# Two more products by seven from chunk 2 on, a new order, and a one-column clear on GpSimd behind each accumulating DMA

## The chip, the cores and the metric

The kernel runs on one core of a Trainium2 chip. The metric is the device time of one execution in microseconds (us); a median of several executions stands for a kernel. The engines of the core are called as in the profile: PE (TensorE, matmuls; PEld is its weight load), DVE (VectorE), ACT (ScalarE), POOL (GpSimd) and SP (SyncE, which issues most DMAs). SBUF is the on-chip memory, PSUM the memory, in banks, into which PE writes its sums.

## The reference

One layer of a gated short-convolution mixer between two RMS norms, in float32. x is 1024 x 1024, `w_in` 1024 x 8192, `w_out` 2048 x 1024.

```python
def short_conv_mixer(u, w_in, conv_w, w_out):
    z, bg, cg, v = jnp.split(u @ w_in.astype(u.dtype), 4, axis=-1)
    y = bg * causal_dwconv(cg * v, conv_w) * jax.nn.silu(z)
    return y @ w_out.astype(u.dtype)

# DEPTH = 1, one short-convolution layer
u = rms_norm(x, pre_norm)
h = x + rms_norm(short_conv_mixer(u, w_in, conv_w, w_out), post_norm)
```

The convolution is causal over the positions, three taps wide, each of the 2048 channels for itself. The other mixer of the file isn't used at this depth.

## The kernel before

**Products by seven.** Both large matrix products are computed as 2 x 2 blocks with seven block products in place of eight (Strassen's scheme in Winograd's form), named a, b, c, e, d, f, g. For `u @ w_in` the work goes by pairs p and chunks c: chunk c has the pairs 2c and 2c+1, sixteen chunks in all. Each float32 operand is split into a high part (rounded to the type fp32r) and a low part (the rest), and each block product is three matmuls: low by high, high by low, high by high. A plain product (`product`) is 12 matmuls of 512 columns. Its weights are tiles named by the letter: `wdh` and `wdl` are the high and the low part for product d, `wch` and `wcl` for c, and so on; the u side lies in tiles such as `u_d`.

**Seven again.** Products b, f and g can be taken by the same scheme once more, over the two pairs of a chunk together: two plain products (24 matmuls of 512 columns) become seven small ones, a' to g', of 6 matmuls of 256 columns (`deep_product`, 42 matmuls). `by_seven(z, c)` says whether product z of chunk c goes so: b from chunk `DEEP` on, f from `DEEP_F`, g from `DEEP_G`, each up to the last chunks. Before, these are 2, 3 and 4. The results go to PSUM tiles such as `px2b`, `pv2f`, `px2g`, which DVE adds to the sums `sna`, `snc`, `sne` in SBUF.

What the small products need: once for the whole kernel the u side, that is, for each of b, f and g eight subtractions on POOL (`deep_subs`, in tiles `deepb`, `deepf`, `deepg`) and the splits of four operands c', e', d', g' (`deep_split`, into tiles such as `ubch_deep`, `ubcl_deep`); for each chunk four sums of 128 x 256 on the weight side (`deep_sums`, tiles `dsb`, `dsf`, `dsg`) and their splits (`deep_prep`, tiles `dwb1h`, `dwb1l` and so on). The table `UNDER` says at which product of which pair the setups of the u side are recorded.

**Splits by bank.** A split takes ACT for the high part and DVE for the low part. Many go by way of one PSUM bank, `beside`, which all of them use in turn: ACT copies the source to the high part and into the bank, and DVE subtracts the high part from the bank. `split_w` takes this way for the weights of a, d and g in chunks whose f goes by seven; `deep_split` in the setups takes it always.

**Transfers.** For the second large product, sums of `w_out`'s blocks are formed in DRAM (`t_d`): SP copies blocks, and sixteen DMAs with an addition (accumulating DMAs), issued by POOL's queue, add others to them. `sums_plan(p0)` lays them out over the pairs from p0 - 1 on, one accumulating DMA for each pair. `TODO` says with which pairs the `tb` tiles are fetched.

**What sets the order.** From `plan.record()` on nothing is issued at once; each operation is recorded by the class `Plan`, with its tiles and an estimated duration. At the end `flush` gives each a due time (`deadlines`), shifts the due times of some by a table (`PLAN["boost"]`, operation number to microseconds), and lays out the instructions of each engine in the order that this gives (`arrange`; `take` moves some POOL operations to DVE). The order of PE is the recorded one. `emit` then issues them by way of `call`, and so every recorded instruction has the line of `call` in the profile (L288).

Of the kernel before, what the change touches and what calls it, by code (L numbers as in the profile page):

```python
# [19 lines left out]
DEEP = 2  # L20
DEEP_F = 3
DEEP_G = 4
# [619 lines left out]
def kernel(  # L642
# [17 lines left out]
    P = 128  # L660
# [1441 lines left out]
```

## Time and profile before

| | us |
|---|---|
| median of 3 executions | 776.41 (775.64 to 776.58) |
| profiled execution, its own time | 776.59 |
| its span in the profile | 774.8 |
| PE busy | 763.8 (99%) |
| DVE busy | 669.9 (86%) |
| ACT busy | 451.2 (58%) |
| POOL busy | 442.6 (57%) |
| start of chunk 2 (product c of pair 4) | 100.01 |
| start of the output product | 618.90 |

A row of a timeline gives the start and the length of an instruction in us, its engine, line and operation, output<-inputs by the program's names without buffer numbers, and in brackets how long the engine was idle before it and what ended that. "PE px L288 <- DVE wdl L288" in the view of waits reads: PE, about to write `px`, waited for DVE's write of `wdl`; then us in total, how many times, the longest. A row of the view of windows gives for a stretch from:to its length and, for each engine, the busy time and the number of instructions.

### The profile page before, as it was taken

The numbers are of one execution on the slowest core, as the hardware profiler recorded it, in microseconds if no ns is written. First come the engines' busy times: TensorE is split into PE (matmuls) and PEld (weight loads), VectorE is DVE, ScalarE is ACT, GpSimd is POOL, SyncE is SP. The second block draws the span as 40 slices with busy tenths as digits, with TensorE's granted clock in tenths as the row PEclk, the third lists the DMA queues.
The fourth block names the chain that finished last, engine by engine and source line by source line (L and its number), as shares of the span: only waits on it lengthen the run. The fifth ranks groups of instructions, "written<-read, shape, count | busy, mean of one in ns | idle before, by whom it ended". The sixth has DMA issues, their size and how long they took to land.

```text
span 774.8 us, 12631 instructions
## 1 busy us (share of the span) xinstructions
PE 763.8 (99%) x4266; PEld 668.0 (86%) x4266; DVE 669.9 (86%) x1009; ACT 451.2 (58%) x861; POOL 442.6 (57%) x397
## 2 busy tenths in 40 slices
PE   8999999999999999999999999999999999999996
PEld 7888888888988898988888888888888889889885
DVE  6899878786989898999899989797899899977993
ACT  7774456675755565756565656556553656564831
POOL 2518994558695859777788687565637100600321
PEclk9999999999999999999999999999999999999999
DMA  9222432354747575556667673724254998666842
GB/s 315 67 55 55 122 111 80 121 161 146 177 136 171 170 161 146 165 143 191 197 177 212 176 203 94 185 81 140 84 163 131 359 388 278 202 224 212 266 142 108
DMA packets 117136, 130.09 MB, mean 168 GB/s; under 512 B 7320, under 2 KB 74704, under 8 KB 116944
## 3 DMA queue, kind: packets, MB, share of 16 engines
q1 hardware_dynamic: 112560, 120.77, 48.4%
q0 software_dynamic: 4352, 8.39, 7.3%
q8 instruction: 33, 0.54, 0.3%
q14 instruction: 31, 0.25, 0.1%
q10 hardware_dynamic: 160, 0.14, 0.0%
HBM read 101.74 MB, written 44.30 MB: 188 GB/s over the span
## 4 chain that ended last, share of the span: by engine, by line
PE 97%; DVE 1%; issue 1%; DMA 1%; ACT 0%; POOL 0%; DVEq 0%; POOLq 0%; ACTq 0%
PE px L288 40%; PE pv L288 15%; PE po_x L288 11%; PE px2b L288 5%; PE px2f L288 3%; PE po_v L288 3%; PE pp L288 3%; PE px2g L288 3%; PE pv2b L288 2%; PE pv2f L288 2%; PE pf_x L288 1%; PE pb_x L288 1%; PE py2b L288 1%; PE py L288 1%; PE pv2g L288 1%
## 5 line engine op out<-in xcount | busy, mean ns | idle before, releaser
L288 PE MATMUL px<-u_d,wdh 128*128 128x512 f32 x248 | 76.7, 390 | 0.0
L288 PE MATMUL px<-u_a,wah 128*128 128x512 f32 x248 | 76.7, 390 | 0.0
L288 PE MATMUL pv<-u_e,weh 128*128 128x512 f32 x248 | 76.6, 390 | 0.0
L288 PE MATMUL px<-u_c,wch 128*128 128x512 f32 x248 | 76.6, 390 | 0.0
L288 ACT COPY beside<-raw 128x512 f32<-128x512 f32 x64 | 37.9, 592 | 37.5 <-DVE wal L288 13.3
L288 PEld LDWEIGHTS px<-u_d,wdh 128*128 128x128 f32 x248 | 46.6, 188 | 9.1
L288 PEld LDWEIGHTS px<-u_c,wch 128*128 128x128 f32 x248 | 46.7, 188 | 9.1
L288 PEld LDWEIGHTS pv<-u_e,weh 128*128 128x128 f32 x248 | 46.6, 188 | 9.0
L288 PEld LDWEIGHTS px<-u_a,wah 128*128 128x128 f32 x248 | 46.7, 188 | 8.9
L288 ACT COPY sna<-px 128x512 f32<-128x512 f32 x30 | 17.6, 586 | 60.4 <-PE px L288 55.6
L288 DVE SCALAR_TENSOR_TENSOR cv<-gpad,cw,cv 128x1024 f32<-128x1024 f32 x32 | 49.4, 1544 | 2.5 <-ACT cv L288 2.3
L288 PE MATMUL px<-u_d,wdl 128*128 128x512 f32 x124 | 48.8, 393 | 0.7 <-DVE wdl L288 0.7
L288 PE MATMUL px<-u_a,wal 128*128 128x512 f32 x124 | 48.6, 392 | 0.0
L288 PE MATMUL px<-u_c,wcl 128*128 128x512 f32 x124 | 48.5, 391 | 0.0
L288 PE MATMUL pv<-u_e,wel 128*128 128x512 f32 x124 | 48.5, 391 | 0.0
L288 POOL TENSOR_TENSOR sf<-raw,sc 128x512 f32<-128x512 f32 x27 | 41.2, 1524 | 10.8 <-issue 5.5
L288 POOL TENSOR_TENSOR raw<-raw,raw 128x512 f32<-128x512 f32 x31 | 45.2, 1459 | 3.5 <-DVE se L288 2.9
L288 POOL TENSOR_TENSOR sc<-se,raw 128x512 f32<-128x512 f32 x24 | 37.3, 1555 | 15.2 <-PE px L288 4.9
L288 POOL TENSOR_TENSOR se<-raw,raw 128x512 f32<-128x512 f32 x22 | 31.1, 1414 | 23.6 <-DVE sna L288 4.7
L288 POOL TENSOR_TENSOR rs_post<-ve_post,minus_half 128x1 f32<-128x1 f32 x7 | 4.9, 704 | 64.5 <-DVE ve_post L288 64.5
L288 ACT COPY snc<-px 128x512 f32<-128x512 f32 x31 | 18.0, 580 | 26.5 <-PE px L288 26.5
L288 POOL TENSOR_TENSOR sne<-snc,sne 128x512 f32<-128x512 f32 x10 | 13.5, 1346 | 33.7 <-ACT snc L288 31.9
(491 smaller groups left out, 2618.2 us busy)
## 6 DMA issues: line engine op xcount, KB each, us to landing
raw<-in_sc_w_in SPq DMA_DIRECT2D x128, 256.0 KB, 3.8
y_d<-cv SPq DMA_DIRECT2D x16, 512.0 KB, 2.7
s_d<-s SPq DMA_DIRECT2D x32, 256.0 KB, 3.2
t_d<-in_sc_w_out POOLq DMA_DIRECT2D x16, 512.0 KB, 7.9
t_d<-in_sc_w_out SPq DMA_DIRECT2D x16, 256.0 KB, 5.2
tb<-in_sc_w_out SPq DMA_DIRECT2D x16, 256.0 KB, 4.0
t_d<-t_d SPq DMA_DIRECT2D x16, 256.0 KB, 4.7
s<-y_d SPq DMA_DIRECT2D x16, 256.0 KB, 3.1
```

Source lines behind the costliest of these rows:

```text
L288: getattr(engine, name)(*(self.plain(a) for a in args), **{k: self.plain(a) for k, a in kw.items()})
```

## The change

`DEEP_F` and `DEEP_G` go from 3 and 4 to 2: product f of chunk 2 and product g of chunks 2 and 3 are taken by seven too. The setups for f and g move with them, so that all twelve operands of the u side are recorded with the products of chunk 2 (`UNDER`, pairs 4 and 5). `sums_plan(10)` becomes `sums_plan(4)`: the copies and the accumulating DMAs for `t_d` begin with pair 3, and before with pair 9. The `tb` fetches start with pair 7 in place of 9. `emit` issues a clear of a 128 x 1 tile on GpSimd behind each DMA of its queue; the planner doesn't know of it. The table of due times is another one. In all there are 54 more matmuls, 22 more rows on DVE's list, 19 more on ACT's, 26 more on POOL's (16 of them clears) and 4 fewer on SP's.

```diff
 DEEP = 2
-DEEP_F = 3
-DEEP_G = 4
+DEEP_F = 2
+DEEP_G = 2
...
     "boost": {
-        0: 3.28, 1: -1.55, 2: -5.74, 3: -3.49, 4: 0.9, 5: -13.11, 6: -1.63, 7: -10.08, 20: 23.61, 21: 13.96,
...
+        0: 0.65, 1: 1.53, 2: -1.38, 5: 25.25, 6: 0.34, 20: 1.61, 22: 15.9, 25: 0.33, 58: 2.17, 59: 3.37,
...
             self.call(op.name[0], op.engine, op.name[1], op.args, op.kw)
+            if op.engine == "gpsimd" and op.name[1] == "dma_start":
+                self.call(op.name[0], "gpsimd", "memset", (self.mark, 0.0), {})
...
-    sums_plan(2 * DEEP_F + 4)
+    sums_plan(4)
...
         ("e", 2 * DEEP - 1): lambda: deep_subs("b", [0]),
         ("f", 2 * DEEP - 1): lambda: deep_subs("b", [1]),
-        ("d", 2 * DEEP): lambda: (deep_split("b", "c'", True), deep_split("b", "e'", True)),
-        ("f", 2 * DEEP): lambda: deep_subs("f", [0, 1]),
-        ("g", 2 * DEEP): lambda: deep_split("b", "d'", True),
-        ("e", 2 * DEEP + 1): lambda: deep_split("b", "g'", True),
-        ("d", 2 * DEEP_F): lambda: deep_split("f", "c'", True),
-        ("a", 2 * DEEP_F + 1): lambda: deep_split("f", "e'", True),
-        ("g", 2 * DEEP_F): lambda: deep_split("f", "d'", True),
-        ("c", 2 * DEEP_F + 1): lambda: deep_split("f", "g'", True),
-        ("e", 2 * DEEP_G - 2): load_ug,
-        ("e", 2 * DEEP_G - 1): lambda: deep_subs("g", [0]),
-        ("a", 2 * DEEP_G): lambda: deep_subs("g", [1]),
-        ("a", 2 * DEEP_G + 1): lambda: deep_split("g", "c'", True),
-        ("c", 2 * DEEP_G + 1): lambda: deep_split("g", "e'", True),
-        ("e", 2 * DEEP_G + 1): lambda: deep_split("g", "g'", True),
-        ("d", 2 * DEEP_G + 1): lambda: deep_split("g", "d'", True),
+        ("c", 2 * DEEP): lambda: (deep_split("b", "c'", True), deep_split("b", "e'", True)),
+        ("e", 2 * DEEP): lambda: (deep_split("b", "d'", True), deep_subs("f", [0, 1])),
+        ("d", 2 * DEEP): load_ug,
+        ("a", 2 * DEEP + 1): lambda: [deep_split("f", i, True) for i in ("c'", "e'", "d'")],
+        ("c", 2 * DEEP + 1): lambda: (deep_split("b", "g'", True), deep_split("f", "g'", True)),
+        ("e", 2 * DEEP + 1): lambda: deep_subs("g", [0, 1]),
+        ("d", 2 * DEEP + 1): lambda: [deep_split("g", i, True) for i in ("c'", "e'", "g'", "d'")],
     }
...
+    plan.mark = small.tile([P, 1], F32, tag="mark", name="mark", bufs=1)
     plan.record()
```

How the new order differs is shown at two places. The first is DVE in chunk 2 around the low part of product d's weights for the chunk's second pair, pair 5 (`wdl`; the numbers behind the names tell the buffers apart). Before:

```order
L288 TENSOR_TENSOR wel_1162<-se_1062,weh_1113 128x512
L288 TENSOR_TENSOR dwb2l_1191<-dsb_2_1126,dwb2h_1151 128x512
L288 TENSOR_TENSOR sna_987<-px2b_1064,sna_987 128x256
L288 TENSOR_TENSOR sna_1173<-pv2b_1177,sna_1173 128x256
L288 TENSOR_TENSOR wdl_1203<-raw_10_974,wdh_1134 128x512
L288 TENSOR_TENSOR wfl_1207<-sf_1145,wfh_1186 128x512
```

In the same place after the change, with f and g by seven:

```order
L258 TENSOR_TENSOR dwf_2_1286<-sf_1134,dwf_2_1286 128x256
L258 TENSOR_TENSOR ubgl_deep<-beside,ubgh_deep 128x512
L258 TENSOR_TENSOR dsg_2_1317<-raw_11_987 128x256
L258 TENSOR_TENSOR dwg0l_1323<-raw_11_852,dwg0h_1311 128x512
L258 TENSOR_TENSOR ufgl_deep<-beside,ufgh_deep 128x512
L258 TENSOR_TENSOR sna_1018<-pv2b_1205,sna_1018 128x256
L258 TENSOR_TENSOR snc_1055<-pv2f_1271,snc_1055 128x256
L258 TENSOR_TENSOR sna_1200<-px2b_1086,sna_1200 128x256
L258 TENSOR_TENSOR wdl_1359<-beside,wdh_1259 128x512
L258 TENSOR_TENSOR dwg1l_1362<-dsg_2_1317,dwg1h_1356 128x512
```

Now two setup splits by the bank (`ubgl_deep`, `ufgl_deep`), a sum and a split for g, and three reads of small products' results stand directly ahead of `wdl`, which itself comes by the bank and no longer from `raw`. In the later chunks of before, where all three products go by seven, `wdl` stands ahead of those reads; this is chunk 5:

```order
L288 TENSOR_TENSOR dwf_5_2494<-sf_2330,dwf_5_2494 128x256
L288 TENSOR_TENSOR dwg0l_2506<-raw_11_1989,dwg0h_2474 128x512
L288 TENSOR_TENSOR wdl_2514<-beside,wdh_2416 128x512
L288 TENSOR_TENSOR sna_2215<-pv2b_2406,sna_2215 128x256
L288 TENSOR_TENSOR sna_2398<-px2b_2309,sna_2398 128x256
L288 TENSOR_TENSOR snc_2291<-pv2f_2464,snc_2291 128x256
```

Against these rows the three reads and `wdl` of the new chunk 2 stand the other way round. The second place is POOL's list around an accumulating DMA, among the sums of g's weight side (`dsg`). Before, in chunk 5:

```order
L288 TENSOR_TENSOR dsg_5_2486<-raw_11_2185 128x256
L288 DMA t_d<-in_sc_w_out 128x2x512
L288 TENSOR_TENSOR dsg_5_2486<-dsg_5_2486,raw_11_1989 128x256
L288 TENSOR_TENSOR dsg_5_2525<-raw_11_1989,raw_11_2185 128x256
L288 TENSOR_TENSOR dsg_5_2525<-raw_11_1989,dsg_5_2486 128x256
L288 TENSOR_TENSOR se_2547<-raw_10_2422,raw_11_2456 128x512
```

After the change, in chunk 4, where such a DMA stands among the same sums:

```order
L258 TENSOR_TENSOR dsg_4_2210<-raw_11_1896 128x256
L258 DMA t_d<-in_sc_w_out 128x2x512
L258 MEMSET mark 128x1
L258 TENSOR_TENSOR dsg_4_2210<-dsg_4_2210,raw_11_1744 128x256
L258 TENSOR_TENSOR dsg_4_2245<-raw_11_1744,raw_11_1896 128x256
L258 TENSOR_TENSOR dsg_4_2245<-raw_11_1744,dsg_4_2210 128x256
```

The clear stands between the DMA and the operation that stood directly behind it before.

140 rows, old and new, of the table PLAN are left out of this document.

## Prediction

> **What bounds the kernel now.** I read the page's busy times first, then the chain of waits, then the waits of PE (TensorE), then the chunks one by one.
>
> ```profile
> PE 763.8 (99%) x4266; PEld 668.0 (86%) x4266; DVE 669.9 (86%) x1009; ACT 451.2 (58%) x861; POOL 442.6 (57%) x397
> PE 97%; DVE 1%; issue 1%; DMA 1%; ACT 0%; POOL 0%; DVEq 0%; POOLq 0%; ACTq 0%
> PE pv2f L288 <- DVE dwf2l L288: 0.9, 1, 0.9
> PE px L288 <- DVE wdl L288: 0.7, 1, 0.7
> ```
>
> PE works 763.8 of 774.8 us and is 97% of the chain that ended last. The last two rows are all that PE waited between 80 and 620 us, in the whole middle of the kernel: once for `dwf2l`, once for `wdl`, both from DVE. So the time falls by the matmuls taken away and by those two waits, and it rises by each place where DVE, at 86%, comes too late for PE.
>
> The next view gives one row per chunk, from its first product c to the next chunk's: from:to and length, then busy time (instructions) of PE, weight load, DVE, ACT, POOL, then granted clock, DMA share and GB/s. The rows are chunks 2 to 6, and chunk 8.
>
> ```profile
> 100.01:137.74 37.73, 37.73 (x187) 32.02 (x186) 28.40 (x42) 23.27 (x49) 26.62 (x22) 1.00 0.25 79
> 137.74:175.07 37.33, 37.33 (x206) 32.50 (x204) 28.62 (x47) 25.69 (x53) 20.12 (x20) 1.00 0.48 149
> 175.07:210.53 35.46, 35.46 (x211) 31.57 (x210) 29.33 (x46) 22.90 (x51) 26.87 (x26) 1.00 0.57 151
> 210.53:249.58 39.05, 37.41 (x224) 33.08 (x223) 35.60 (x50) 21.53 (x43) 29.05 (x27) 1.00 0.58 167
> 249.58:286.50 36.92, 36.92 (x224) 32.99 (x223) 33.15 (x50) 21.26 (x41) 27.67 (x26) 1.00 0.63 162
> 323.40:360.30 36.90, 36.90 (x224) 32.96 (x223) 34.64 (x52) 22.53 (x43) 25.82 (x27) 1.00 0.56 159
> ```
>
> Each product taken by seven shortens a chunk (37.73 with b, 37.33 with b and f, 36.90 with all three; chunk 4 is short because the g of its last pair ends in chunk 5). Only chunk 5 loses: 39.05 against 36.92. DVE can be busy 34.64 of 36.90 us, 94%, and PE still loses nothing.
>
> **The change part by part.** *Matmuls.* Product f of chunk 2 and g of chunks 2 and 3 go by seven: three more. The chain's pieces price them:
>
> ```profile
> 107.04 2.75 PE px L288 x12
> 109.79 2.72 PE pv L288 x12
> 105.61 0.71 PE px2b L288 x6
> 640.66 2.87 PE pb_x L288 x24
> ```
>
> A plain product of 12 matmuls of 512 columns is 2.72 to 2.75 us; a small one, 6 of 256 columns, 0.71, and 24 matmuls of that size take 2.87, 120 ns each, 0.72 for 6. Two plain products (5.47, a 2.75 and a 2.72) become seven small ones (7 x 0.72 = 5.04): 0.40 to 0.43 each time. From the chunks it is the same: chunks 2 to 5 without chunk 5's loss are 37.73 + 37.33 + 35.46 + 36.92 = 147.44, and the new pattern is 35.46 + 3 x 36.90 = 146.16. That is **-1.28 us**, all on PE's path, with 54 more matmuls (4320). The Trainium skill (TensorE: Matmul & The Clock Gate, Back-to-back issue gap) gives N/2.4 + 2.5 ns for a matmul at full clock, by which 24 of 512 columns against 42 of 256 would save 0.59 us each time, 1.8 in all, and the sum below would be 0.5 lower. The trace's 120 ns against 109 for the small ones decides for 1.28.
>
> *Chunk 5's loss.* Here are DVE, then POOL (GpSimd), then PE in that stretch; the columns are start, length, engine, work.
>
> ```profile
> 231.99 3.25 DVE L288 TENSOR_TENSOR dwb<-raw,dwb 128x256 fp32r<-128x256 f32 x1
> 235.16 0.68 DVE L288 TENSOR_TENSOR dwf2l<-beside,dwf2h 128x512 fp32r<-128x512 f32 x1
> 235.76 0.89 DVE L288 TENSOR_TENSOR dwf<-sf,dwf 128x256 fp32r<-128x256 f32 x1
> 236.57 1.77 DVE L288 TENSOR_TENSOR dwg0l<-raw,dwg0h 128x512 fp32r<-128x512 f32 x1
> 238.27 0.68 DVE L288 TENSOR_TENSOR wdl<-beside,wdh 128x512 fp32r<-128x512 f32 x1
> ...
> 230.41 1.15 POOL L288 DMA_DIRECT2D t_d<-in_sc_w_out  x1
> 231.16 1.17 POOL L288 TENSOR_TENSOR dsg<-dsg,raw 128x256 f32<-128x256 f32 x1
> 231.87 1.15 POOL L288 TENSOR_TENSOR dsg<-raw,raw 128x256 f32<-128x256 f32 x1
> 232.57 1.14 POOL L288 TENSOR_TENSOR dsg<-raw,dsg 128x256 f32<-128x256 f32 x1
> ...
> 235.89 0.39 PE L288 MATMUL pv2f<-u_f,dwf2l 128*128 128x256 f32 x1 [0.90 <-DVE dwf2l L288]
> 239.00 0.50 PE L288 MATMUL px<-u_d,wdl 128*128 128x512 f32 x1 [0.74 <-DVE wdl L288]
> ```
>
> `dwb`, a subtraction of two SBUF tiles, takes 3.25 us, through three POOL operations on end, all begun without a gap behind an accumulating DMA that POOL issues. What follows on DVE is late: `dwf2l` ends at 235.84 and `wdl` at 238.95, and PE starts 0.05 us after each. The 0.90 and 0.74 and 0.49 of slowed matmuls make 2.13 (39.05 - 36.92). The same subtraction took 0.41 in the next chunk, where another operation was caught behind the next such DMA:
>
> ```profile
> 269.82 1.16 POOL L288 DMA_DIRECT2D t_d<-in_sc_w_out  x1
> ...
> 271.96 2.01 DVE L288 TENSOR_TENSOR dsg<-raw,raw 128x256 f32<-128x256 f32 x1
> 273.89 0.41 DVE L288 TENSOR_TENSOR dwb<-raw,dwb 128x256 fp32r<-128x256 f32 x1
> ...
> 342.77 1.82 DVE L288 TENSOR_TENSOR dwb<-raw,dwb 128x256 fp32r<-128x256 f32 x1
> ```
>
> The last row is the third such case, two chunks on; behind the other thirteen of these DMAs I find none as long.
>
> After the change a clear of one column stands between the DMA and the POOL operation behind it. It reads no tile, and I take it that DVE gets its turn there; and the order around every such DMA is new besides. So **-2.13**, with ends 0 (the hold stays and again meets a thin place) and -2.13. The Trainium skill (SBUF — State Buffer, Who interferes with whom) says that a DVE instruction with two SBUF inputs contends with a GpSimd instruction that reads SBUF, and not with one that only writes; that agrees with `dwb` here, but a lock for one instruction would hold it for 1.17, not 3.25.
>
> *The clears themselves.* The nearest row is a clear of the same size in the head:
>
> ```profile
> 0.74 0.10 POOL L288 MEMSET eps_t<- 128x1 f32 x1 [0.29 <-POOLq L2088]
> 95.43 1.12 DVE L288 TENSOR_TENSOR wcl<-sc,wch 128x512 fp32r<-128x512 f32 x1 [1.84 <-ACT wch L288]
> 100.01 0.39 PE L288 MATMUL px<-u_c,wcl 128*128 128x512 f32 x1
> ```
>
> Sixteen of 0.10 us are 1.6 us of POOL, which is idle 43% of the span: 0. If a clear waited for the DMA's issue (1.15 us) POOL would lose 18 us, still under its 332 idle us. The accumulating DMAs and SP's copies ahead of them come three chunks earlier, the fetches for `tb` one: DMA engines are 0.25 busy in chunk 2 and 0.63 in chunk 6 without a wait of PE, so 0 too; on POOL's queue each puts 0.7 us (230.41 to 231.16) ahead of `dsg` and `se`, which POOL has spare time for (26.62 of 37.73 busy in chunk 2).
>
> *The crowded chunk 2.* All twelve setups of the small products' u sides, before spread over chunks 2, 3 and 4, now lie in chunk 2. In the new order three DVE reads of product b's and f's results stand ahead of `wdl` of the chunk's second pair. The last of them reads what the small product d' of b leaves; that product is over at 24.22 us from the chunk's start by PE's own pace, and product d, which needs `wdl`, is due at 24.94. Reads start 0.19 us behind the end of the product, as here:
>
> ```profile
> 230.85 0.42 DVE L288 TENSOR_TENSOR snc<-px2f,snc 128x256 f32<-128x256 f32 x1 [1.80 <-PE px2f L288]
> ```
>
> That product's successor began at 230.66. Then 0.34 for the read, 0.68 for `wdl`, 0.05 to PE: 24.22 + 1.26 = 25.48, a wait of 0.54 that no speed elsewhere removes. Above it counts DVE's work. The groups of DVE between 100 and 500 us, with mean ns, price its rows:
>
> ```profile
> L288 DVE SCALAR_TENSOR_TENSOR cv<-gpad,cw,cv 128x1024 f32<-128x1024 f32 x20 | 30.6, 1532 | 0.8 <-ACT cv L288 0.6
> L288 DVE TENSOR_TENSOR wel<-se,weh 128x512 fp32r<-128x512 f32 x21 | 19.9, 948 | 0.3 <-POOL dsb L288 0.3
> L288 DVE TENSOR_TENSOR dwb<-raw,dwb 128x256 fp32r<-128x256 f32 x11 | 9.1, 824 | 0.3 <-ACT dwb L288 0.3
> L288 DVE TENSOR_TENSOR sna<-px2b,sna 128x256 f32<-128x256 f32 x43 | 17.8, 414 | 6.0 <-PE px2b L288 6.0
> ```
>
> From the chunk's start to that `wdl` stand 45 DVE rows: 19 of 512 columns that read PSUM (0.68, as `wdl` above) and 10 of 256 (0.41), 8 and 7 that read SBUF alone (0.95 and 0.8), one convolution tap (1.53): 12.9 + 4.1 + 7.6 + 5.6 + 1.5 = 31.75 in all; less 0.08 of overlap each, 28.15. DVE has 24.94 plus its lead, 3.46 us (`wcl` ends at 96.55, PE takes it at 100.01): 28.4. At the 94% that chunk 8 showed, 28.15 becomes 29.95, a wait of 1.5; at 85%, 33.1, one of 4.7. I take **+1.5**, ends 0.5 and 4.7, since the 94% is shown without loss. From there on PE's pause gives DVE the time back: the whole of chunk 2 needs 36.1 us of DVE, chunk 3 31.6 of 36.8.
>
> Sum: 776.59 - 1.28 - 2.13 + 1.5 = 774.68. The profiled execution (span 774.8, 1.79 around it) is 0.18 above the median of 776.41, so **774.5** there.
>
> **The rivals.** *Within 0.2%* (0.2% is 1.55 us, about what a measurement of this kernel can tell): the hold goes on and one of the sixteen DMAs again meets a place without slack, 774.5 + 2.1 = 776.6; or DVE is short in chunk 2 by 3.5 to 4.7, 776.5 to 777.7. For it speak the three long operations above, of sixteen such DMAs; against it that POOL's row behind each is now a write without a read.
>
> *Slower: the bank `beside`.* One PSUM bank serves all splits by bank in turn: ACT copies into it, DVE subtracts, then ACT may copy again. Between `wdl` of chunk 2's first pair and that of its second stand 14 turns in about 26 us, 1.86 each. The shortest turn in the trace is 1.34:
>
> ```profile
> 123.08 0.69 DVE L288 TENSOR_TENSOR ubgl_deep<-beside,ubgh_deep 128x512 fp32r<-128x512 f32 x1 [2.75 <-ACT ubgh_deep L288]
> 124.42 0.69 DVE L288 TENSOR_TENSOR wal<-beside,wah 128x512 fp32r<-128x512 f32 x1 [0.66 <-ACT beside L288]
> ```
>
> and most are longer, as nothing hurried them. With ACT and DVE both full a turn also stands behind other work in both queues. At 2.5 us the 14 take 35, 9 over: 774.5 - 1.5 + 9 = 782. From 2.24 us a turn the kernel is slower by over 0.2%.
>
> *The clears do nothing.* The DMAs now start in chunk 2, where DVE has no slack; one hold of `dwb`'s size (3.25 - 0.42 = 2.8) ahead of `wdl` there, and the loss of 2.13 not won elsewhere: 774.5 + 2.8 + 2.1 = 779.4.
>
> *Cheaper than I think.* The matmuls by the formula, and only the floor of 0.5 at `wdl`: 774.5 - 0.5 - 1.0 = 773.0.
>
> **How the numbers follow.** Forecast and the cheaper case together 0.48 (773.0 to 774.8); within 0.2% 0.27; the bank 0.15; the clears without effect 0.10. Hence faster 0.48, same 0.27, slower 0.25. The likeliest case has 773.5 to 775.5. The range leaves out the upper half of the bank's case and a little below: 772.8 to 780.0.
>
> **What would show it.** Right: 4320 matmuls; chunk 2 of 35.5 plus one wait of 1 to 2 us at the second `wdl`, then three chunks of 36.9; no DVE subtraction of 256 columns over 2 us behind an accumulating DMA. Wrong: several waits of PE in chunk 2 for tiles that come from `beside` (the bank); a DVE operation of 3 us in chunk 2 or 3 (the clears); or new waits in chunks 6 and later, where the order changed as well and I count nothing.

## The result and the profile after

The changed kernel takes 777.72 us (median of 19 executions, 777.04 to 779.13) and the kernel before 776.42 (median of 19) beside it: ratio 1.0015, 95% interval 1.0009 to 1.0021. It is slower by 1.3 us. That is 0.15%, small but clear of the scatter, and it is not the way that was forecast. The profiled spans are 776.0 and 774.8.

These are the busy times, the chain by engine, and all waits of PE between 80 and 640 us of the changed kernel:

```profile
PE 763.2 (98%) x4320; PEld 669.7 (86%) x4320; DVE 670.8 (86%) x1031; ACT 457.7 (59%) x880; POOL 461.3 (59%) x423
PE 94%; DVE 2%; ACT 1%; issue 1%; DMA 1%; POOL 0%; POOLq 0%; DVEq 0%; ACTq 0%
PE pv2f L258 <- DVE dwf2l L258: 3.0, 2, 1.6
PE px L258 <- DVE wdl L258: 0.4, 1, 0.4
PE px L258 <- ACT sna L258: 0.2, 1, 0.2
```

The 4320 matmuls are there, but PE waits 3.6 us in place of 1.6, and most of it again for `dwf2l`, now twice. By chunks (from:to and length, then busy us of PE, weight load, DVE, ACT and POOL, clock, DMA share, GB/s), chunks 2 to 5 and then chunk 9, which begins at 359.91 (the expectations below call it chunk 8):

```profile
99.98:136.55 36.57, 35.99 (x211) 31.69 (x210) 35.15 (x56) 31.33 (x78) 28.31 (x30) 1.00 0.69 180
136.55:173.47 36.92, 36.92 (x224) 32.98 (x223) 34.53 (x52) 23.02 (x45) 31.78 (x30) 1.00 0.57 150
173.47:212.23 38.76, 37.16 (x224) 33.01 (x223) 32.49 (x51) 21.92 (x44) 30.62 (x30) 1.00 0.57 158
212.23:249.15 36.92, 36.92 (x224) 32.98 (x223) 31.53 (x52) 21.46 (x42) 28.03 (x27) 1.00 0.61 162
359.91:398.42 38.51, 37.16 (x225) 33.01 (x223) 34.93 (x52) 22.18 (x43) 30.86 (x31) 1.00 0.59 157
```

Chunk 5 no longer loses. Chunk 4 now loses 38.76 - 36.92 = 1.84, chunk 9 1.59, and chunk 2 36.57 - 35.46 = 1.11. Chunks 2 to 5 took 149.57 before and take 149.17, 0.40 less; with chunk 9 that makes +1.19, and the spans differ by 1.2. The other chunks up to 14 are as long as before.

Here is DVE in chunks 4 and 9 of the changed kernel, and then POOL:

```profile
195.85 2.69 DVE L258 TENSOR_TENSOR dwb<-raw,dwb 128x256 fp32r<-128x256 f32 x1
198.47 0.41 DVE L258 TENSOR_TENSOR dwf<-sf,dwf 128x256 fp32r<-128x256 f32 x1
198.80 0.68 DVE L258 TENSOR_TENSOR dwf2l<-beside,dwf2h 128x512 fp32r<-128x512 f32 x1
...
381.68 2.78 DVE L258 TENSOR_TENSOR dwb<-raw,dwb 128x256 fp32r<-128x256 f32 x1
384.39 0.68 DVE L258 TENSOR_TENSOR dwg0l<-raw,dwg0h 128x512 fp32r<-128x512 f32 x1
384.99 0.68 DVE L258 TENSOR_TENSOR dwf2l<-beside,dwf2h 128x512 fp32r<-128x512 f32 x1
```

```profile
380.84 1.17 POOL L258 DMA_DIRECT2D t_d<-in_sc_w_out  x1
381.57 0.55 POOL L258 MEMSET mark<- 128x1 f32 x1
381.63 1.18 POOL L258 TENSOR_TENSOR dsg<-dsg,raw 128x256 f32<-128x256 f32 x1
382.33 1.16 POOL L258 TENSOR_TENSOR dsg<-raw,raw 128x256 f32<-128x256 f32 x1
383.03 1.14 POOL L258 TENSOR_TENSOR dsg<-raw,dsg 128x256 f32<-128x256 f32 x1
```

It is the picture that chunk 5 gave before the change: `dwb` is held for 2.7 us while POOL runs its `dsg` behind an accumulating DMA. The clear stands there, and it is overlapped by the operation behind it (381.57 + 0.55 is past 381.63). A third hold of this kind lies at the start of chunk 2, behind the first accumulating DMA (101.11); it is an operation on the tile `cv`:

```profile
101.39 2.99 DVE L258 TENSOR_TENSOR cv<-cv,sna 128x512 f32<-128x512 f32 x1
```

One regularity in the traces gave the theory for the experiments. An overlap of more than 0.3 us between a POOL operation and the next occurs 13 times in the kernel before and 35 times in the changed one (100 to 600 us; 17 of them are left when the clears are taken away, since most of the clears overlap), and each time in an unbroken run behind an accumulating DMA, never elsewhere. The DVE operations that were held longest, 3.25 before and 2.99, 2.78 and 2.69 after, all begin in such runs. **Theory H:** the DMA starts a run of POOL operations without a gap, which lasts until POOL has to wait; a DVE operation on two SBUF tiles that comes into it is held, and a clear is one more member of the run. **Rival C**, the prediction's own: the clear lets DVE in, and it only doesn't reach far enough. **Rival O:** DVE is too late in these places whatever POOL does.

### The profile page after: what moved, and what is told of

Its sections match the earlier page's. It is cut to its first block, busy times and chain, and to the rows that moved or that the text cites. A ratio compares the mean times of both kernels' runs of the same rounds, so it can differ in the third digit from the quotient of the medians.

```text
span 776.0 us, 12801 instructions
## 1 busy us (share of the span) xinstructions
PE 763.2 (98%) x4320; PEld 669.7 (86%) x4320; DVE 670.8 (86%) x1031; ACT 457.7 (59%) x880; POOL 461.3 (59%) x423
## 4 chain that ended last, share of the span: by engine, by line
PE 94%; DVE 2%; ACT 1%; issue 1%; DMA 1%; POOL 0%; POOLq 0%; DVEq 0%; ACTq 0%
PE px L258 38%; PE pv L258 14%; PE po_x L258 11%; PE px2b L258 5%; PE px2g L258 3%; PE px2f L258 3%; PE po_v L258 3%; PE pp L258 3%; PE pv2f L258 2%; PE pv2b L258 2%; PE pf_x L258 1%; PE pb_x L258 1%; PE py2b L258 1%; PE pv2g L258 1%; PE py L258 1%
## 5 line engine op out<-in xcount | busy, mean ns | idle before, releaser
L258 ACT COPY beside<-raw 128x512 f32<-128x512 f32 x67 | 39.7, 592 | 29.6 <-DVE dwf2l L258 9.4
L258 POOL TENSOR_TENSOR sf<-raw,sc 128x512 f32<-128x512 f32 x28 | 44.2, 1580 | 4.3 <-PE px L258 3.4
L258 POOL TENSOR_TENSOR rs_post<-ve_post,minus_half 128x1 f32<-128x1 f32 x7 | 6.5, 941 | 67.2 <-DVE ve_post L258 67.2
L258 POOL TENSOR_TENSOR sc<-se,raw 128x512 f32<-128x512 f32 x25 | 34.7, 1389 | 18.8 <-PE px2b L258 5.1
L258 POOL TENSOR_TENSOR ry_f<-ry_f 128x256 f32<-128x256 f32 x4 | 14.5, 3650 | 38.5 <-DMA ry_f<-s_d 38.5
L258 ACT COPY sne<-pv 128x512 f32<-128x512 f32 x31 | 18.1, 584 | 21.5 <-PE pv L258 21.5
```

The costliest lines, as they stand in the source:

```text
L258: getattr(engine, name)(*(self.plain(a) for a in args), **{k: self.plain(a) for k, a in kw.items()})
```

## The experiments

### The clears: taken away, added to the kernel before, and more of them

```diff
             self.call(op.name[0], op.engine, op.name[1], op.args, op.kw)
-            if op.engine == "gpsimd" and op.name[1] == "dma_start":
-                self.call(op.name[0], "gpsimd", "memset", (self.mark, 0.0), {})
```

> The changed kernel without the sixteen clears, everything else the same. Theory of the run (H): behind an accumulating DMA POOL's operations follow each other without a gap until POOL has to wait, a DVE subtraction of SBUF tiles that comes into such a run is held to its end, and a clear changes nothing: the two subtractions dwb near 196 and 382 us still take 2.6 to 3.3, time as the changed kernel's 777.7, within 0.6. Theory of the clear (C, the prediction's): the clear gives DVE a turn, so without it more operations are held, at least one more PE wait of 1 us or more appears, 779 or more. If the clears only cost (POOL 0.55 each), 777.7 or a little below, 777.0.

777.40 us, ratio to the kernel before 1.0012 (1.0003 to 1.0020); both waits for `dwf2l` are there, 1.42 and 1.34. In chunk 9 `dwb` took 2.78, to the hundredth as with the clear. In chunk 4 it took 1.42, but the subtraction behind it, `dwf`, was held as well, 1.50, and `dwf2l` came nearly as late: the hold was split over two operations, where H had all of it on `dwb`. Without the clears nothing got worse.

The same three lines, put into the kernel before:

> The kernel before, with a clear of one column behind each of its sixteen accumulating DMAs and nothing else changed. H (POOL's operations behind such a DMA hold DVE to the end of the run, and a clear in the run changes nothing): dwb near 232 us still takes about 3, chunk 5 about 39, time 776.4, within 0.6. C (the clear gives DVE a turn): dwb at most 1.8, chunk 5 loses 0.7 at most, 775.0 or less.

776.55 us, ratio 1.0004 (0.9995 to 1.0012). POOL and then DVE in chunk 5 of this run:

```profile
230.77 1.17 POOL L288 DMA_DIRECT2D t_d<-in_sc_w_out  x1
231.50 0.55 POOL L288 MEMSET mark<- 128x1 f32 x1
231.56 1.19 POOL L288 TENSOR_TENSOR dsg<-dsg,raw 128x256 f32<-128x256 f32 x1
```

```profile
232.33 3.33 DVE L288 TENSOR_TENSOR dwb<-raw,dwb 128x256 fp32r<-128x256 f32 x1
235.58 0.68 DVE L288 TENSOR_TENSOR dwf2l<-beside,dwf2h 128x512 fp32r<-128x512 f32 x1
```

With the clear in place `dwb` is held for 3.33 where it was 3.25, and chunk 5 takes 39.11.

Then a clear behind each operation of the two bad runs:

```diff
+        n, left = 0, 0
...
             if op.engine == "gpsimd" and op.name[1] == "dma_start":
+                n += 1
+                left = 4 if n in (5, 14) else 1
+            if op.engine == "gpsimd" and left:
+                left -= 1
                 self.call(op.name[0], "gpsimd", "memset", (self.mark, 0.0), {})
```

> The changed kernel with a clear also behind each of the three dsg operations that follow the fifth and the fourteenth accumulating DMA, six clears more. H: a clear in the run is one more operation without a gap; both dwb take 2.7 or more, 777.7 to 778.5. C in its stronger form (a clear, which reads nothing, lets DVE in wherever it stands): both dwb take at most 1.8, as behind one POOL operation, and the waits of 1.60 and 1.35 shrink by about 1 each: 775.5 to 776.

777.84 us, ratio 1.0017 (1.0008 to 1.0026). In chunk 9 the clears interleave with the `dsg` and all overlap:

```profile
381.22 0.55 POOL L258 MEMSET mark<- 128x1 f32 x1
381.28 1.18 POOL L258 TENSOR_TENSOR dsg<-dsg,raw 128x256 f32<-128x256 f32 x1
381.96 0.54 POOL L258 MEMSET mark<- 128x1 f32 x1
382.01 1.16 POOL L258 TENSOR_TENSOR dsg<-raw,raw 128x256 f32<-128x256 f32 x1
```

```profile
381.32 2.87 DVE L258 TENSOR_TENSOR dwb<-raw,dwb 128x256 fp32r<-128x256 f32 x1
```

In chunk 4 `dwb` took 1.52 and `dwf` 1.50, nearly as in the run without any clear, and PE waited 1.51 there and 1.44 in chunk 9. So the 1.8 that C asked for is met by `dwb` in chunk 4, but not through the clears, and its gain of 1 us in each place isn't there. C falls in both its forms: the clear is without effect, for good or ill, within about 0.6 us.

### The DMAs: left out, or moved out of the run

Theory O asks whether the accumulating DMAs matter at all. Left out in `emit`, with their clears, in the changed kernel and in the kernel before:

```diff
+            if op.engine == "gpsimd" and op.name[1] == "dma_start":
+                continue
             self.call(op.name[0], op.engine, op.name[1], op.args, op.kw)
```

> The changed kernel without its sixteen accumulating DMAs and their clears (the sums for the second product are not formed: a part of the computation is left out). H: no POOL operation begins over 0.3 us before the end of the one ahead, no DVE subtraction between 100 and 600 us takes over 1.8; PE's waits for dwf2l are gone, 774.3; if the holds in chunk 2 count too, 773.8. O: 777.2 to 777.7, since the POOL operations themselves stay.

773.50 us, ratio 0.9959 (0.9947 to 0.9972), 0.3 below the lower expectation of H and far from O. Chunks 4 and 9 take 36.92, and chunk 2 takes 36.12 in place of 36.57: the hold there costs 0.45. So the DMAs cost the changed kernel 1.84 + 1.59 + 0.45 = 3.88 us in its chunks.

> The kernel before without its sixteen accumulating DMAs (their sums are left out). H: chunk 5 at 36.92, no PE wait between 80 and 620 us, 776.4 - 2.1 = 774.3; so the three products by seven and the new order alone, against the changed kernel without these DMAs (773.5), would be worth 0.6 to 0.8, which is 1.28 less the 0.66 of chunk 2. If before loses something else there: 775 or more.

774.21 us, ratio 0.9969 (0.9958 to 0.9981), and no wait of PE between 80 and 640 us. In the changed kernel the same query gives one:

```profile
PE px L258 <- DVE wdl L258: 0.4, 1, 0.4
```

No overlap over 0.3 us is left on POOL in either. Without these DMAs the change is worth 774.21 - 773.50 = 0.7 us, as expected: three products by seven (1.28) less what chunk 2 loses (36.12 - 35.46 = 0.66). The intervals of the two ratios overlap, so the times alone don't settle 0.7; the chunks do better, 0.57 less from chunk 2 to chunk 13.

On the real computation, the DMA of one bad run is issued seven POOL operations later, behind `sf`, where POOL then waits for ACT; in the kernel before the third DMA, in the changed kernel the fifth and the fourteenth:

```diff
+MOVE = {3: 7}            # changed kernel: {5: 7, 14: 7}
...
+            if op.engine == "gpsimd" and op.name[1] == "dma_start":
+                n += 1
+                if n in MOVE:
+                    held, left = op, MOVE[n]
+                    continue
             self.call(op.name[0], op.engine, op.name[1], op.args, op.kw)
+            if op.engine == "gpsimd" and held is not None:
+                left -= 1
+                if left == 0:
+                    self.call(held.name[0], "gpsimd", held.name[1], held.args, held.kw)
+                    held = None
```

> The kernel before, with its third accumulating DMA alone issued seven POOL operations later, behind sf of the same chunk. H: dwb near 232 takes 0.4 to 1.2, chunk 5 36.92, both waits of PE gone: 776.4 - 2.1 = 774.3. O (DVE too late there anyway): 776 or more. A third way, seen once already when two DMAs were moved: another of the DMAs takes over the hold, 775 to 775.5.

774.53 us, ratio 0.9978 (0.9969 to 0.9986). DVE in chunk 5 of the kernel before, with one DMA moved:

```profile
231.94 0.42 DVE L290 TENSOR_TENSOR dwb<-raw,dwb 128x256 fp32r<-128x256 f32 x1
232.33 0.69 DVE L290 TENSOR_TENSOR dwf2l<-beside,dwf2h 128x512 fp32r<-128x512 f32 x1
```

`dwb` falls from 3.25 to 0.42 and chunk 5 from 39.05 to 36.92, with nothing changed on DVE. That settles O: DVE was not late by itself. Chunk 6 loses 0.36 now (37.28); the fourth DMA, which had stood idle on POOL for 2.46 us, starts in it.

> The changed kernel with two of its sixteen accumulating DMAs (the fifth and the fourteenth) and their clears issued seven POOL operations later, behind sf, where POOL then waits for ACT. H: both dwb take 0.4 to 1.2, both waits of PE for dwf2l (1.60 and 1.35) are gone, chunks 4 and 8 take 36.9: 777.72 - 1.84 - 1.59 = 774.3. Theory of the full DVE (O: DVE is too late there anyway, the DMA has no part): nothing or under 0.5 us is won, 777.2 to 777.7.

775.30 us, ratio 0.9988 (0.9979 to 0.9997), 1 us above the expectation. Chunks 4 and 9 take 36.92 and both waits for `dwf2l` are gone. But chunk 5 now takes 37.90: the sixth DMA stood idle on POOL, and the run behind the seventh, later than it was, caught `dwb`; PE waits 0.7 for `wdl` there. POOL and DVE of this run:

```profile
203.02 1.18 POOL L260 DMA_DIRECT2D t_d<-in_sc_w_out  x1
...
213.16 1.18 POOL L260 DMA_DIRECT2D t_d<-in_sc_w_out  x1 [4.40 <-issue]
```

```profile
233.62 2.49 DVE L260 TENSOR_TENSOR dwb<-raw,dwb 128x256 fp32r<-128x256 f32 x1
```

### Is it any DMA of POOL's?

The sixteen DMAs as plain copies, in the same places, with the clears:

```diff
+            if op.engine == "gpsimd":
+                op.kw.pop("accum_op", None)
             self.call(op.name[0], op.engine, op.name[1], op.args, op.kw)
```

> The changed kernel with its sixteen DMAs on POOL's queue as plain copies, without the addition (that part of the computation is left out); order and clears as they are. If it is the issue of a DMA by POOL that starts a run without gaps (H): overlapped POOL operations behind them as before, dwb near 196 and 382 at 2.6 to 2.9, 777.7. If it is the addition in the transfer: no runs, 773.5 to 774.

774.28 us, ratio 0.9972 (0.9962 to 0.9982): the expectation under H was wrong here. POOL and DVE in chunk 4:

```profile
192.89 0.73 POOL L258 DMA_DIRECT2D t_d<-in_sc_w_out  x1
193.62 0.12 POOL L258 MEMSET mark<- 128x1 f32 x1
193.67 0.76 POOL L258 TENSOR_TENSOR dsg<-dsg,raw 128x256 f32<-128x256 f32 x1
194.38 0.75 POOL L258 TENSOR_TENSOR dsg<-raw,raw 128x256 f32<-128x256 f32 x1
```

```profile
195.08 1.03 DVE L258 TENSOR_TENSOR dwb<-raw,dwb 128x256 fp32r<-128x256 f32 x1
```

The plain DMA's row is 0.73 long and not 1.17, the clear 0.12 and not 0.55, the `dsg` 0.75 and not 1.17, and nothing overlaps. The operations start 0.70 apart in both cases; only behind the accumulating form do they end 0.4 later than the next one starts. So H needs one word more: the runs with overlaps come from the accumulating DMA, not from any DMA that POOL issues. A plain one isn't free, though. Chunks 4 and 9 still lose 0.19 and 0.41, and in chunk 2 `cv`, which came 0.30 us behind the start of the plain DMA, was held through the DMA, the clear and the operation behind them:

```profile
101.05 2.50 DVE L258 TENSOR_TENSOR cv<-cv,sna 128x512 f32<-128x512 f32 x1
```

Without any DMA there it takes 1.66 and with the accumulating one 2.99. Why the accumulating form leaves POOL in that state no run here shows.

### Moving many of them

With nine DMAs moved into POOL's waits, chosen from the trace without DMAs:

> The changed kernel without clears, with nine of the sixteen accumulating DMAs (1, 3, 5, 7, 9, 10, 12, 14, 16) issued later, each ahead of a POOL operation that waited in the run without these DMAs. All DMAs are there. H: no dwb, dwf or dwg0l over 1.8 near a DMA, chunks 3 to 13 at 36.92, only the wait for wdl in chunk 2 left: 773.5 as without the DMAs, up to 774.0 if DMA 2 still costs. If it is the transfers themselves that hold DVE, and not where they are issued: 775 or more.

787.58 us, ratio 1.0143 (1.0125 to 1.0162). In this run the tenth DMA, moved by eight operations, had come behind the SP copies that read its result, so what they copy lacks that addition. With `wdl` first in chunk 2 as well (the last diff of this part):

> As the run with nine DMAs moved, and in chunk 2 wdl of the second pair stands ahead of the three reads of small products' results on DVE. If the order is what PE waits for there (0.41 of wait, 0.66 of chunk 2's length over 35.46): that wait is gone, 0.6 less than with the nine moved, 773.0. If DVE's work up to there is what comes late (27 of 28 us needed): a wait of 0.2 to 0.4 stays, 773.3 to 773.5.

789.61 us, ratio 1.0173 (1.0155 to 1.0190), with the tenth DMA in the same place. With that DMA moved by two operations only:

> The changed kernel without clears, with the same nine accumulating DMAs issued later, only the tenth by two POOL operations and not by eight: in the run that moved it by eight it had come behind the SP copies that read its result. H: every DMA of the nine stands ahead of a POOL wait, no DVE subtraction near them over 1.8, chunks 3 to 13 at 36.92, one PE wait (wdl in chunk 2) left: 773.5 as without the DMAs, up to 774.0. If the transfers themselves hold DVE: 775 or more.

793.73 us, ratio 1.0223 (1.0197 to 1.0250), and still slow. Two rows of POOL and one of DVE tell where it begins:

```profile
211.71 1.19 POOL L260 DMA_DIRECT2D t_d<-in_sc_w_out  x1 [3.73 <-issue]
...
250.47 1.19 POOL L260 DMA_DIRECT2D t_d<-in_sc_w_out  x1 [5.77 <-DMA raw<-in_sc_w_in]
```

```profile
309.76 6.03 DVE L260 TENSOR_TENSOR dwg0l<-raw,dwg0h 128x512 fp32r<-128x512 f32 x1
```

These two DMAs were due (POOL was done with the operation ahead of them) 5.4 and 4.8 us behind the start of the DMA before and started 9.2 and 10.6 us behind it; until then POOL stood idle, with its whole list behind them. POOL's waits were then no longer where the trace without DMAs had them, and the tenth DMA started a run of five operations, which held `dwg0l` for 6.03. The spacing isn't all of it. In chunk 9, which takes 44.60, SP waits for the landing of the twelfth DMA, moved by five operations, before it copies what that DMA added to, and three loads of `raw` stand behind those copies on SP's queue:

```profile
SPq L260 <- DMA t_d<-in_sc_w_out: 7.6, 1, 7.6
377.52 0.69 DVE L260 TENSOR_TENSOR se<-raw,raw 128x512 f32<-128x512 f32 x1 [8.92 <-DMA raw<-in_sc_w_in]
```

The first row is SP's wait between 350 and 368 us, the second DVE's wait for a load of `raw`. From 100 to 520 us SP's waits of this kind are 23.5 us here and 8.6 in the changed kernel. How the loss divides between the two paths no run separates.

> As the run before, and wdl of pair 5 ahead of the three DVE reads in chunk 2. If the order there is the whole cause of that wait: chunk 2 at 35.5, 0.6 less than the run before, 772.9. If DVE's amount of work up to there comes late too: a wait of 0.2 to 0.4 stays, 773.2 to 773.5.

792.38 us, ratio 1.0197 (1.0182 to 1.0211). The time is of no use, but chunk 2, ahead of all that, took 36.12 in the run before and 35.53 in this.

Last, three DMAs alone, with 10 us or more kept between those that the moves brought closer in chunks 4 and 5:

```diff
+MOVE = {5: 4, 7: 3, 14: 7}
```

> The changed kernel without clears, with only three accumulating DMAs issued later: the fifth by four POOL operations, the seventh by three, the fourteenth by seven. In the traces so far a POOL DMA that is due less than about 10 us behind the one before stood idle on POOL (3.7 and 4.4 us marked issue, 5.8 in another), and here the fifth and sixth and the seventh and eighth keep 12 us. If the slow runs with nine moved come from that spacing (S) and the holds from runs behind accumulating DMAs (H): no PE wait for dwf2l, chunks 3 to 13 at 36.92, chunk 2 36.6: 777.7 - 3.4 = 774.3. If moving DMAs costs by itself: over 776.5.

774.78 us, ratio 0.9981 (0.9972 to 0.9991), 0.5 above the expectation. Chunks 4 and 5 take 36.92; chunk 9, where the fourteenth DMA stands, loses 0.37. And with the first DMA moved by three and, in chunk 2, `wdl` ahead of the three reads (below the dots stands DVE's list, not code):

```diff
+MOVE = {1: 3, 5: 4, 7: 3, 14: 7}
...
+wdl_1359<-beside,wdh_1259 128x512
 sna_1018<-pv2b_1205,sna_1018 128x256
 snc_1055<-pv2f_1271,snc_1055 128x256
 sna_1200<-px2b_1086,sna_1200 128x256
-wdl_1359<-beside,wdh_1259 128x512
```

> As the run before, the first accumulating DMA three POOL operations later as well, and wdl of pair 5 ahead of the three DVE reads in chunk 2. In the two slow runs chunk 2 took 36.12 with the first DMA moved and 35.53 with wdl first as well. By S and H: all chunks without loss, 774.3 - 0.5 - 0.6 = 773.2; if one of the four moves makes a new wait: 774 or more.

773.94 us, ratio 0.9972 (0.9961 to 0.9983): faster than both kernels, though 0.7 above the expectation. It has no wait of PE between 80 and 640 us, and only chunk 3 is longer than forecast (37.06). All sixteen transfers are there, so the transfers as such cost PE little; what counts is where they are issued. Its chunks 2, 4 and 9:

```profile
99.89:135.41 35.52, 35.52 (x211) 31.57 (x209) 31.45 (x56) 29.93 (x74) 28.16 (x27) 1.00 0.69 179
...
172.47:209.39 36.92, 36.92 (x225) 32.98 (x223) 32.40 (x51) 21.89 (x44) 30.59 (x28) 1.00 0.57 165
...
357.07:393.99 36.92, 36.92 (x225) 32.98 (x223) 32.87 (x52) 22.04 (x42) 30.62 (x28) 1.00 0.57 150
```

The span, 771.5, is 3.3 below that of the kernel before: the forecast's 1.28 and 2.13 together are 3.41.

## Why the prediction was wrong

It said faster, 774.5, and the kernel is slower, 777.72. By its own terms:

- **Matmuls, -1.28: right.** 4320 of them; the chunks without a loss have the forecast pattern, 36.92 and, in the last version, 35.52 for chunk 2: 35.52 + 3 x 36.92 = 146.28 against 147.44, which is -1.16. The 1.8 estimated from the Trainium skill's formula (TensorE: Matmul & The Clock Gate, Back-to-back issue gap), which that section gives for an isolated matmul, isn't seen.
- **Chunk 5's loss, -2.13: the step that failed.** "It reads no tile, and I take it that DVE gets its turn there" was an inference from one property of the clear, with no row that showed a clear in such a run. The clear does nothing (1.0004 in the kernel before with it, 1.0012 against 1.0015 in the changed kernel without it). Chunk 5's loss went, since the new order brought no `dwb` into that run, and came back as 1.84 in chunk 4, 1.59 in chunk 9 and 0.45 in chunk 2. In place of -2.13 the term was -2.13 + 1.84 + 1.59 + 0.45 = +1.75, outside both ends that the prediction gave it (0 and -2.13): with sixteen such DMAs and a new order, more than one could meet a thin place.
- **`wdl` in chunk 2, +1.5: the size was off.** Chunk 2 lost 1.11, but only 0.66 of it by the order of the rows (36.12 against 35.46, with 0.41 of wait for `wdl`). The floor of 0.54, worked out from the order alone, was near, and the count of DVE's work above it wasn't needed. The read ahead of `wdl` waited for PE, so DVE was on time:

```profile
124.91 0.43 DVE L258 TENSOR_TENSOR sna<-px2b,sna 128x256 f32<-128x256 f32 x1 [0.15 <-PE px2b L258]
125.25 0.68 DVE L258 TENSOR_TENSOR wdl<-beside,wdh 128x512 fp32r<-128x512 f32 x1
```

With `wdl` ahead of the reads that wait is gone (36.12 to 35.53). The other 0.45 belongs to the term above: behind the hold of `cv` (2.99) DVE and ACT are late, PE waits 0.17 for `sna`, and matmuls are slowed. In the run with nine DMAs moved (the first by three operations, the tenth by two) that loss is gone (36.12), and `cv` takes 1.66:

```profile
101.32 1.66 DVE L260 TENSOR_TENSOR cv<-cv,sna 128x512 f32<-128x512 f32 x1
```

- **The rivals.** No wait of PE comes from the bank `beside`; up to the second `wdl` of chunk 2 DVE waited for a copy into it for 0.2 us in all. "The clears do nothing", to which the prediction gave the smallest chance, named the mechanism and was right about a DVE operation of 3 us in chunk 2; but that hold (2.99, on `cv`) cost 0.45 and not 2.8, and the loss of chunk 5 was won, so that 779.4 was too high. "Within 0.2%" had the mechanism too, as one DMA that again meets a place without slack (2.1); there were two such places, 3.43 together, and the small one in chunk 2. One of them lies in chunk 9, where the prediction says that it counts nothing.
- **Clears and moved DMAs, 0 on POOL:** the clears are 0.55 each there, not the 0.10 of the row that priced them, and cost nothing that the runs resolve.

The sum with the measured terms: -1.28 + 0.66 + 1.75 = +1.13; the chunks and the spans differ by 1.2, the rest being 36.92 in place of 36.90 for three chunks.

## What to carry to other kernels

When a stall is explained by what two engines do at the same moment, look for how often the same pattern stands elsewhere in the trace before costing its removal; here the new order moved such a pattern and didn't remove it. A wait that follows from the order of two rows (a read that needs PE, ahead of a tile that PE needs) can be priced from the order and two latencies, and here that floor was nearly all. In this kernel an accumulating DMA on POOL's queue did little harm ahead of an operation on which POOL has to wait (773.94); many of them moved at once came too close together and made the copies and loads behind them late (793.73).

## What the runs showed of the hardware

- Behind an accumulating DMA (row of 1.17 us) POOL's operations of 256 columns follow each other 0.70 us apart with rows of 1.17, until POOL waits; behind a plain DMA in the same place (0.73) the rows are 0.75. A DVE operation on two SBUF tiles that came into such a run was held for up to 3.33 us, and for 6.03 and 6.05 in two of the runs with nine DMAs moved. Outside such runs the longest row of this kind between 100 and 600 us is 1.79 in the kernel before and the changed one; behind a plain DMA one took 2.50.
- A clear of one column takes 0.12 us on POOL outside such a run and 0.55 inside, and made no hold shorter. The Trainium skill (SBUF — State Buffer, Who interferes with whom) has a two-input DVE instruction contend only with a GpSimd instruction that reads SBUF. By that alone one might expect an opening at each clear; with a clear behind each `dsg` the run shows `dwb` held for 2.87, and the rows of the clears overlap those of the `dsg`.
- An accumulating DMA that was due 1.2 to 6.1 us behind the one before stood idle on POOL and started 6.5 to 10.6 us behind it; those due 7.3 us or more behind didn't wait, so the "about 10" of the expectation above is too many. From issue to landing such a DMA takes 6.7 to 8.2 us (medians of the runs), so it may be the transfer before that it waits for. No run tests this.
